# When the next head's adding transfers start, and when the output projections' rows are loaded and split

## The chip, the cores and the metric

The kernel runs on one core of a Trainium2 chip. The metric is the device time of one execution in microseconds (us). Five engines work side by side, each on its own list of instructions, in order: TensorE (PE: matrix products; PEld is its loading of weights), VectorE (DVE), ScalarE (ACT), GpSimd (POOL) and SyncE (SP), which here only issues transfers. GpSimd and ScalarE issue transfers too. The order of each list is made when the kernel is built; when the instructions run is settled by semaphores.

## What is computed

Two decoder layers on 512 tokens of width 2048, in float32. The first layer is differential attention with 8 heads, the second a gated RWKV-7. Both end in an output projection that is added to the input:

```python
def diff_attention_mixer(h, cos, sin, w_in, q_gain, k_gain, ..., w_out, lambda_init):
    proj = h @ w_in                       # 512 x 2048 by 2048 x 8192
    q, k, v, gate = jnp.split(proj, 4, axis=-1)
    ...
    q = apply_rope(rms_norm(q, q_gain), cos, sin)
    k = apply_rope(rms_norm(k, k_gain), cos, sin)
    ...
    o = causal_diff_attention(q, k, v, lam)
    o = rms_norm(o, subln_w) * (1.0 - lambda_init)
    o = o.reshape(B, T, DA_WIDTH).astype(h.dtype) * jax.nn.silu(gate)
    return o @ w_out
...
def rwkv7_mixer(...):
    p = h @ w_in
    ...
    y = wkv7_scan(rh, heads(decay), kh, vh, -kk, kk * ah)
    ...
    y = y.reshape(B, T, RW_WIDTH).astype(h.dtype) * jax.nn.silu(g)
    return y @ w_out, v_first
...
for i in range(DEPTH):                    # DEPTH = 2
    hn = rms_norm(x, norm_w[i])
    x = x + (diff_attention_mixer(...) if i % 2 == 0 else rwkv7_mixer(...)[0])
```

## The kernel before

**Splits.** Every product is made of three matmuls on halves: a value is rounded to a high half by a cast on ScalarE, and VectorE subtracts it from the value to give the low half. For weights, `split_w` does this (lines 109 and 110) or, in the first layer's heads, `Seven.split` (lines 600 and 601: `wh`, `wl`). Rows of the left side are split by `split_row` (lines 474 and 475: `hH`, `hL`). Weights are loaded as raw tiles (`wraw`, three buffers, 512 KB for two blocks of 128 rows) by SyncE; four buffers each hold high and low halves.

**A head of the first layer.** `Seven.head` makes the projection of one head (heads 1 to 7; head 0 goes another way) with products on sums of weight blocks in place of some plain products. A weight sum is made by transfers: SyncE loads one block into a tile, then GpSimd issues a transfer that adds another block to it in memory (`fetch` with `add=True`, line 571; plain loads are line 573). Six pairs of blocks of such sums live in the tile `T`; they carry the next head's first product. `prime(h + 1)` loads `T` by SyncE in three groups (512 KB each), `prime(h + 1, True)` adds to it by GpSimd, three transfers again.

The end of a head runs as follows, in the program's order. The S1 product: three groups, each a raw tile loaded by SyncE and added to by GpSimd. Then the combining step of line 640 (`take`, on VectorE, at a higher priority than the splits). Then the first group of the S4 product, with its own raw tile (the "first S4 load"). Then, for heads 1 to 6, `prime(h + 1, True)`, the three adding transfers for the next head, inside `tc.issue_after(g.m.ins)`, where `g.m` is the last matmul. Then the plain products on blocks 12 and 13, and 14 and 15, each pair from one raw tile. Then the other two groups of S4.

`tc.issue_after(ins)` puts the instructions that it encloses behind `ins` in the list of the engine of `ins`: only those that are on that engine. `high_priority` moves instructions ahead in the order that the builder chooses.

While a head's products run, the attention of the head before is interleaved by a `Chain`: after so many matmuls (`delay`, then the step's own gap) it issues its next step. In the attention, scores go to `sc`, line 415 makes the weights `p` on VectorE, line 421 turns them on TensorE, line 445 turns the result `yt`.

**The output projections.** `unit_tok` multiplies 16 rows of the attention's result (16 blocks of 128 by 512 tokens) with `w_out`, in 8 weight groups of two blocks, 24 matmuls a group, and calls `more(n, m)` three times in each group, with growing `n`. The rows lie in device memory (`yd`, `yd2`). Before, `split_rows` loads and splits 14 rows ahead of the projection: it issues a load and a split for each row in one go. In the first layer, rows 0 to 3 and 8 to 11 go through parts of `Tt` (the place of `T`), the others through four `t1` tiles, and splits from row 8 on stand behind the last gate's instructions. The last head's attention runs meanwhile (`Chain` with delay 4, gap 21; seven steps); it gives rows 14 and 15. In the second layer the rows go through eight tiles of one buffer each, and the last pair's recurrence runs meanwhile.

The rest of both projections uses sums again (`sum_forms`, `seven`) and isn't touched.

Of the kernel before, what the change touches and what calls it, by code (L numbers as in the profile page):

```python
# [13 lines left out]
F32 = mybir.dt.float32  # L14
# [9 lines left out]
P = 128  # L24
D = 2048
T = 512
KT = D // P
NT = T // P
NH = 8
# [51 lines left out]
class Halves:  # L81


    def __init__(self, parts, n):
        self.parts, self.n = parts, n
# [5 lines left out]
@urgent  # L91
def split_w(g, block, kg, cols, k0, raw=None):


    nc = g.nc
    held = raw is not None and block is not None
    if raw is None:
        raw = g.wraw.tile([P, kg, cols], F32, name="wraw", tag="wraw")
        load_w(g, raw, block, k0, slice(0, kg))
    n = kg // 2  # L100
    his, los = [], []
    for k in range(0, kg, n):
        hi = g.wh.tile([P, n, cols], F32R, name="wh", tag="wh")
        lo = g.wl.tile([P, n, cols], F32R, name="wl", tag="wl")
        with ExitStack() as after:
            if held and k0 + k < 4:
                for ins in g.made[k0 + k - 1] if k0 + k else [g.made_prm]:
                    after.enter_context(g.tc.issue_after(ins))
            nc.scalar.copy(hi[:], raw[:, k : k + n])  # L109
            nc.vector.tensor_sub(lo[:], raw[:, k : k + n], hi[:].bitcast(F32))  # L110
        his.append(hi)
        los.append(lo)
    return Halves(his, n), Halves(los, n)
# [356 lines left out]
def split_row(g, yr):  # L470
    nc = g.nc
    hh = g.hp.tile([P, T], F32R, name="hH", tag="hH")
    hl = g.hp.tile([P, T], F32R, name="hL", tag="hL")
    nc.scalar.copy(hh[:], yr)
    g.rowsplit = nc.vector.tensor_sub(hl[:], yr, hh[:].bitcast(F32)).ins
    return hh, hl


def split_rows(g, src, tags, bufs, n=KT, late=KT, behind=(), first=()):

    out = []
    for k in range(n):
        i = k % (2 * len(first)) if first else k
        yr = first[i] if i < len(first) else g.work.tile([P, T], F32, name="yr", tag=tags[k % len(tags)], bufs=bufs)[:]
        g.nc.sync.dma_start(out=yr, in_=src[k * P : (k + 1) * P, :])
        with ExitStack() as after:
            for ins in behind if k >= late else ():
                after.enter_context(g.tc.issue_after(ins))
            out.append(split_row(g, yr))
    return out  # L490


class Tokens:
# [24 lines left out]
class Seven:  # L518
# [3 lines left out]
    def __init__(self, g, aps):  # L522
        self.g, self.made = g, 0
        self.win = aps["da_w_in"]
        tags = [t for t in LOW for _ in range(LOW[t])]
        self.S = {n: [g.low.tile([P, 2, 2, 256], F32R, name=n, tag=t, bufs=LOW[t]) for t in tags[3 * i : 3 * i + 3]]
                  for i, n in enumerate(("S1", "S2", "S4"))}
        self.T = g.work.tile([P, KP, 512], F32, name="T", tag="T", bufs=1)
# [50 lines left out]
    def raw(self, n, k0, half, h, also=None):  # L579

        with self.ahead:
            raw = self.g.wraw.tile([P, n, 512], F32, name="wraw", tag="wraw")[:]
            self.fetch(raw, k0, half, h)
            if also:
                self.fetch(raw, *also, h, add=True)
        return raw
# [6 lines left out]
    def split(self, raw):  # L593

        g, out = self.g, []
        with self.ahead:
            for k in range(raw.shape[1]):
                hi = g.wh.tile([P, 512], F32R, name="wh", tag="wh")
                lo = g.wl.tile([P, 512], F32R, name="wl", tag="wl")
                g.nc.scalar.copy(hi[:], raw[:, k])  # L600
                g.nc.vector.tensor_sub(lo[:], raw[:, k], hi[:].bitcast(F32))  # L601
                out.append((hi, lo))
        return out
# [38 lines left out]
    def head(self, h):  # L642

        g, A, B, U, W, T = self.g, self.A, self.B, self.U, self.W, self.T
        top, low = (lambda k: self.rows(k, 0)), (lambda k: self.rows(KP + k, 0))
        tile_of = lambda k, n: T[:, k : k + n]
        more = lambda k0, half: lambda k, n: self.add(k, n, k0, half, h)
        q = QK(g)
        self.product(B, lambda k: self.rows(k, 1), h, tile_of, True, then=more(0, 0))
        self.product(A, top, h, lambda k, n: self.raw(n, k, 0, h), True)  # L650
        self.copy(W, B)
        self.product(B, low, h, lambda k, n: self.raw(n, KP + k, 0, h), True, end=False)
        self.copy(q.t1s[:2], A)
        self.product(A, lambda k: self.form("S2", k), h, tile_of, False, then=more(KP, 0), end=False)
        self.copy(U, A)
        self.plain(0, h, ((0, B, False, True), (1, A, False, False)))
        self.take(q.t1s[:2], q.t1s[:2], B)
        self.product(A, lambda k: self.rows(KP + k, 1), h, tile_of, False)
        if h + 1 < NH:
            self.prime(h + 1)  # L660
        for t in range(2):
            rope(g, q, t)
        self.take(q.t1s[2:], A, W)
        self.product(B, lambda k: self.form("S1", k), h, lambda k, n: self.raw(n, k, 0, h, (k, 1)), True)
        for t in range(2, NT):
            rope(g, q, t)
        norm_qk(g, q)
        qkT = head_qkT(g)
        Chain(g, keys(g, q, qkT, 10), 52)
        last = lambda k, n: self.raw(n, KP + k, 1, h)  # L670
        s4 = lambda k: self.form("S4", k)
        self.take(U, B, U, ALU.subtract)
        self.product(A, s4, h, last, True, GROUPS[:1])
        if h + 1 < NH:
            with g.tc.issue_after(g.m.ins):
                self.prime(h + 1, True)
        self.plain(1, h, ((0, A, False, False), (1, B, True, True)))
        self.take(W, U, W, ALU.subtract)
        self.product(A, s4, h, last, False, GROUPS[1:])
        vg = VG(g)  # L680
        for c in list(g.chains):
            c.finish(g)
        self.take(W, W, B)
        self.take(U, U, A)
        with g.tc.high_priority(offset=AHEAD if h == NH - 1 else 0):
            for t, x in ((2, W[0]), (3, W[1]), (0, U[0]), (1, U[1])):
                vg.convert(g, t, x)
        return qkT + (q.sq, vg)
# [151 lines left out]
def layer0(g, aps):  # L840
# [3 lines left out]
    with ExitStack() as cx:  # L844
# [22 lines left out]
        with tc.high_priority(offset=AHEAD):  # L867
            xs += [xp.tile([P, NT, 512], F32, name=f"x{cb}") for cb in range(4)]
            g.first += [(g.wraw.tile([P, 2, 512], F32, name="wraw", tag="wraw"), i == 0) for i in range(3)]
            at = lambda k, n: (xs[k // 4], slice(k * P, (k + n) * P), slice(k % 4 * P, (k % 4 + n) * P))  # L870
            load_x(*at(0, 1))
            warmed = warm_up(5)
            g.prm_a = load_rows(g, [(0, 32, aps["norm_w"].rearrange("l (k p) -> (l k) p", p=P))], 32, nc.scalar)
            first = load_first(0, slice(0, 1), nc.scalar)
            on = g.const.tile([P, 1], F32, name="on")
            nc.vector.memset(on[:], 0.0)
            with tc.issue_after(first):
                nc.scalar.copy(on[:], on[:])
            load_x(*at(1, 1))
            load_first(0, slice(1, 2))  # L880
            load_x(*at(2, 1))
            load_first(2, slice(0, 2))
            load_x(*at(3, 1))
            load_x(*at(4, 2))
            load_first(4, slice(0, 2))
            for k in range(6, KT, 2):
                load_x(*at(k, 2))
# [39 lines left out]
    with ExitStack() as cx:  # L927
# [16 lines left out]
            Chain(g, attention(g, h - 1, *before, 37), 28 if h > 1 else 1)  # L944
            before = u.head(h)
        Tt = g.work.tile([P, KP, 512], F32, name="Tt", tag="T", bufs=1)
        rows = split_rows(g, g.yd, ("t1",), 4, KT - 2, 8, g.gated, [Tt[:, k] for k in range(4)])
        ch = Chain(g, attention(g, NH - 1, *before, 21, rows, Tt[:, 4:6]), 4)

        def all_rows(n, _):  # L950
            if n >= KT - 1:
                ch.finish(g)

# [694 lines left out]
def layer1(g, aps):  # L1648
    nc, tc = g.nc, g.tc
    with ExitStack() as cx:  # L1650
# [74 lines left out]
                gated(g, j - 1, pairs[j - 1], gts[0], True)  # L1725

        gts.append(gate(g, j, proj(3, j, behind=[(24, last_but_one)]), "E"))
        rows = split_rows(g, g.yd2, ("r", "k", "th0", "th1", "l", "f", "xH", "xL"), 1, j - 1)

        def all_rows(n, _):  # L1730
            if n >= 4 and len(rows) == KT - 2:
                rows.append(split_row(g, gts[0][:]))
            if n >= KT and len(rows) < KT:
                p.chain.finish(g)
                finish_y(g, j, p)
                gated(g, j, p, gts[1], True)
                rows.append(split_row(g, gts[1][:]))
# [110 lines left out]
```

## Time and profile before

| | us |
|---|---|
| three runs, median | 2096.42 |
| lowest, highest | 2092.53, 2097.5 |
| profiled execution, its own time | 2097.94 |
| its span in the profile | 2096.2 |
| TensorE busy | 2071.3 |
| VectorE busy | 1663.4 |
| ScalarE busy | 1250.0 |
| GpSimd busy | 401.8 |

The profile is of one execution, and its span is counted from its first to its last instruction. In a row of a group or a timeline stand start and duration in us, the engine, the line of the kernel, the operation and, as out<-in, the tiles that it writes and reads; in brackets the idle time of the engine before it and what ended that. In a list of waits stand the total, the number and the longest. "SPq" and the like mean the queue of an engine that issues transfers. The granted TensorE clock was 0.998 of full speed. Heads 1 to 7 take the stretch from about 97 to 750 us, the first layer's output projection begins at 750, the second layer's ends the span.

### The profile page before, as it was taken

The numbers are of one execution on the slowest core, as the hardware profiler recorded it, in microseconds if no ns is written. First come the engines' busy times: TensorE is split into PE (matmuls) and PEld (weight loads), VectorE is DVE, ScalarE is ACT, GpSimd is POOL, SyncE is SP. The second block draws the span as 40 slices with busy tenths as digits, with TensorE's granted clock in tenths as the row PEclk, the third lists the DMA queues.
The fourth block names the chain that finished last, engine by engine and source line by source line (L and its number), as shares of the span: only waits on it lengthen the run. The fifth ranks groups of instructions, "written<-read, shape, count | busy, mean of one in ns | idle before, by whom it ended". The sixth has DMA issues, their size and how long they took to land.

```text
span 2096.2 us, 35298 instructions
## 1 busy us (share of the span) xinstructions
PE 2071.3 (99%) x12008; PEld 1708.4 (81%) x12008; DVE 1663.4 (79%) x4353; ACT 1250.0 (60%) x3005; POOL 401.8 (19%) x698
## 2 busy tenths in 40 slices
PE   9999999999999999999999999999999999999999
PEld 8888878888887878888778888888888888877887
DVE  5978777787877886576888888888888888887645
ACT  5766665666666664446666666666666666655333
POOL 0110101101010000101233332233333322343001
PEclk9999999999999999999999999999999999999999
DMA  6577868677776766652212222222222222245565
GB/s 200 147 181 178 188 177 196 165 188 179 184 189 181 176 228 198 167 117 93 83 55 79 79 81 71 87 79 79 79 79 79 78 77 75 85 129 173 194 162 119
DMA packets 101781, 280.71 MB, mean 134 GB/s; under 512 B 12544, under 2 KB 29072, under 8 KB 101600
## 3 DMA queue, kind: packets, MB, share of 16 engines
q1 hardware_dynamic: 68064, 198.90, 29.3%
q0 software_dynamic: 19104, 63.55, 16.5%
q10 hardware_dynamic: 14432, 16.01, 2.2%
q8 instruction: 94, 1.54, 0.3%
q14 instruction: 87, 0.71, 0.1%
HBM read 262.42 MB, written 15.99 MB: 133 GB/s over the span
## 4 chain that ended last, share of the span: by engine, by line
PE 86%; DVE 7%; ACT 2%; DMA 2%; issue 1%; POOL 0%; ACTq 0%; DVEq 0%; POOLq 0%
PE pp L118 65%; PE pt L118 6%; DMA wraw<-in_da_w_in_dram 2%; PE gp L1340 1%; PE sc L118 1%; PE sm L1559 1%; PE sm L1581 1%; PE lora L118 1%; DVE wl L601 1%; PE sm L1572 1%; PE o L118 1%; PE z L118 1%; DVE wl L110 1%; PE Y L1605 1%; PE pt L359 1%
## 5 line engine op out<-in xcount | busy, mean ns | idle before, releaser
L118 PE MATMUL pp<-hH,wh 128*128 128x512 f32 x1024 | 416.7, 407 | 0.0
L118 PE MATMUL pp<-hL,wh 128*128 128x512 f32 x1024 | 412.3, 403 | 0.0
L118 PE MATMUL pp<-hH,wl 128*128 128x512 f32 x1024 | 411.8, 402 | 0.0
L109 ACT CAST wh<-wraw 128x512 fp32r<-128x512 f32 (+1 forms) x412 | 253.9, 617 | 198.4 <-PE pp L118 100.0
L118 PE MATMUL pp<-wl,hH 128*128 128x512 f32 x932 | 365.9, 393 | 4.2 <-DVE wl L601 4.2
L118 PE MATMUL pp<-wh,hH 128*128 128x512 f32 x932 | 366.7, 394 | 0.5 <-ACT wh L600 0.5
L110 DVE TENSOR_TENSOR wl<-wraw,wh 128x512 fp32r<-128x512 f32 (+1 forms) x412 | 286.0, 695 | 101.4 <-ACT wh L109 97.1
L118 PE MATMUL pp<-wh,hL 128*128 128x512 f32 x932 | 365.6, 392 | 0.0
L118 PEld LDWEIGHTS pp<-hH,wh 128*128 128x128 f32 x1024 | 192.8, 188 | 37.8 <-issue 2.3
L118 PEld LDWEIGHTS pp<-hH,wl 128*128 128x128 f32 x1024 | 193.1, 189 | 32.9
L118 PEld LDWEIGHTS pp<-hL,wh 128*128 128x128 f32 x1024 | 193.2, 189 | 31.3
L118 PEld LDWEIGHTS pp<-wl,hH 128*128 128x128 f32 x932 | 175.2, 188 | 42.4 <-DVE wl L601 7.6
L118 PEld LDWEIGHTS pp<-wh,hH 128*128 128x128 f32 x932 | 175.1, 188 | 36.8 <-ACT wh L600 1.9
L118 PEld LDWEIGHTS pp<-wh,hL 128*128 128x128 f32 x932 | 175.1, 188 | 35.7
L600 ACT CAST wh<-wraw 128x512 fp32r<-128x512 f32 x224 | 138.4, 620 | 105.5 <-PE pp L118 69.0
L601 DVE TENSOR_TENSOR wl<-wraw,wh 128x512 fp32r<-128x512 f32 x224 | 151.5, 687 | 51.9 <-ACT wh L600 51.3
L1567 POOL COPY SA<-VS 64x64 f32<-64x64 f32 x224 | 75.7, 338 | 520.9 <-DVE VS L1585 464.5
L118 PE MATMUL pp<-wh,S 128*128 128x512 f32 x504 | 162.7, 394 | 0.0
L571 POOL DMA_DIRECT2D T<-in_da_w_in_dram x63 | 53.8, 869 | 493.2 <-DVE wl L601 400.8
L1433 DVE SCALAR_TENSOR_TENSOR tmpl<-LT,n,Tm 128x60 f32<-128x60 f32 (+24 forms) x496 | 135.5, 273 | 13.3
L1436 DVE TENSOR_TENSOR Tm<-Tm,tmpl 128x60 f32<-128x60 f32 (+24 forms) x496 | 105.7, 213 | 13.6
L600 ACT CAST wh<-T 128x512 fp32r<-128x512 f32 x126 | 77.8, 618 | 54.0 <-PE pp L118 53.8
(372 smaller groups left out, 3971.0 us busy)
## 6 DMA issues: line engine op xcount, KB each, us to landing
wraw<-in_rw_w_in_dram SPq DMA_DIRECT2D x128, 512.0 KB, 3.7
wraw<-in_da_w_in_dram SPq DMA_DIRECT2D x127, 512.0 KB, 4.3
T<-in_da_w_in_dram POOLq DMA_DIRECT2D x63, 512.0 KB, 6.6
wraw<-in_da_w_out_dram SPq DMA_DIRECT2D x26, 512.0 KB, 4.4
wraw<-in_rw_w_out_dram SPq DMA_DIRECT2D x26, 512.0 KB, 4.0
T<-in_da_w_in_dram SPq DMA_DIRECT2D x21, 512.0 KB, 6.4
wraw<-in_da_w_in_dram POOLq DMA_DIRECT2D x21, 512.0 KB, 7.4
yr<-yd SPq DMA_DIRECT2D x20, 256.0 KB, 3.3
```

The source lines that it names most:

```text
L109: nc.scalar.copy(hi[:], raw[:, k : k + n])
L110: nc.vector.tensor_sub(lo[:], raw[:, k : k + n], hi[:].bitcast(F32))
L118: m = nc.tensor.matmul(out, a, b, start=s, stop=e, skip_group_check=skip)
L359: nc.tensor.transpose(pt[:, c * P : (c + 1) * P], t1s[t][:, c * P : (c + 1) * P], g.ident[:])
L571: self.g.nc.gpsimd.dma_start(out=raw, in_=src, accum_op=ALU.add)
L600: g.nc.scalar.copy(hi[:], raw[:, k])
L601: g.nc.vector.tensor_sub(lo[:], raw[:, k], hi[:].bitcast(F32))
L1340: m = nc.tensor.matmul(gp[h][:, i * P : (i + 1) * P], BK[r_, c0 + i, :, :], p.AR[r_, c0 + i, :, :], start=True, stop=True)
L1433: st = nc.vector.scalar_tensor_tensor(tt, LT[:, i : i + 1, i + 1 :].to_broadcast([P, s, n]), n2[:, i : i + 1], Tm[:, 0:s, i : i + 1].to_br ...
L1436: nc.vector.tensor_add(Tm[:, 0:s, i + 1 :], Tm[:, 0:s, i + 1 :], tt)
L1559: nc.tensor.matmul(sm[:, 0:P], both(p.G[:, c, 0]), both(VS[:, c]), start=True, stop=True)
L1567: nc.gpsimd.tensor_copy(p.SA[r_, c - 1, :], VS[r_, c, h, :])
```

## The change

First, in the heads: the program remembers the last raw tile that was fetched (`self.fetched`; where it is used, the first S4 load). Ahead of the next head's three adding transfers, GpSimd copies one column of that tile into a small tile (`mark`, 128 by 1, which nothing else needs by then), and the transfers are put behind this copy, on the same engine, in place of behind a matmul. So the copy waits until the tile has landed, and the transfers wait for the copy.

Second, in both output projections: `split_rows` gives way to a class `Feed`. It loads six rows and splits four at the start; at each call of `more(n, m)` it splits on to row n + 1 and loads on to row n + 7, and VectorE's part of these splits is put behind the last weight split (`g.split`). With n = 2, 3, 4 in the first group and 4, 5, 6 in the second, the rest of the 14 rows is split from the first to the fifth weight group. The first layer's condition on the last gate is gone. The last attention's delay is 12 instead of 4 and its gap 22 instead of 21.

```diff
-            nc.vector.tensor_sub(lo[:], raw[:, k : k + n], hi[:].bitcast(F32))
+            g.split = nc.vector.tensor_sub(lo[:], raw[:, k : k + n], hi[:].bitcast(F32)).ins
...
-def split_rows(g, src, tags, bufs, n=KT, late=KT, behind=(), first=()):
-
-    out = []
-    for k in range(n):
-        i = k % (2 * len(first)) if first else k
-        yr = first[i] if i < len(first) else g.work.tile([P, T], F32, name="yr", tag=tags[k % len(tags)], bufs=bufs)[:]
-        g.nc.sync.dma_start(out=yr, in_=src[k * P : (k + 1) * P, :])
-        with ExitStack() as after:
-            for ins in behind if k >= late else ():
-                after.enter_context(g.tc.issue_after(ins))
-            out.append(split_row(g, yr))
-    return out
+class Feed:
+    def __init__(self, g, src, n, home):
+        self.g, self.src, self.n, self.home, self.raw, self.rows = g, src, n, home, [], []
+        self.load(6)
+        self.split(4)
+
+    def load(self, upto):
+        for k in range(len(self.raw), min(upto, self.n)):
+            self.raw.append(self.home(k))
+            self.g.nc.sync.dma_start(out=self.raw[k], in_=self.src[k * P : (k + 1) * P, :])
+
+    def split(self, upto, after=None):
+        for k in range(len(self.rows), min(upto, self.n)):
+            with self.g.tc.issue_after(after) if after else ExitStack():
+                self.rows.append(split_row(self.g, self.raw[k]))
+
+    def __call__(self, n):
+        self.split(n + 2, self.g.split)
+        self.load(n + 8)
...
             self.fetch(raw, k0, half, h)
+            self.fetched = raw
...
         if h + 1 < NH:
-            with g.tc.issue_after(g.m.ins):
+            landed = g.nc.gpsimd.tensor_copy(self.mark[:], self.fetched[:, 0, 0:1])
+            with g.tc.issue_after(landed.ins):
                 self.prime(h + 1, True)
...
-        rows = split_rows(g, g.yd, ("t1",), 4, KT - 2, 8, g.gated, [Tt[:, k] for k in range(4)])
-        ch = Chain(g, attention(g, NH - 1, *before, 21, rows, Tt[:, 4:6]), 4)
+        feed = Feed(g, g.yd, KT - 2, lambda k: g.work.tile([P, T], F32, name="yr", tag="t1", bufs=4)[:] if k & 4 else
+                    Tt[:, k % 4])
+        rows = feed.rows
+        ch = Chain(g, attention(g, NH - 1, *before, 22, rows, Tt[:, 4:6]), 12)
 
         def all_rows(n, _):
+            feed(n)
             if n >= KT - 1:
                 ch.finish(g)
...
-        rows = split_rows(g, g.yd2, ("r", "k", "th0", "th1", "l", "f", "xH", "xL"), 1, j - 1)
+        feed = Feed(g, g.yd2, KT - 2, lambda k: w.tile([P, T], F32, name="yr", bufs=1, tag=(
+            "r", "k", "th0", "th1", "l", "f", "xH", "xL")[k % 8])[:])
+        rows = feed.rows
 
         def all_rows(n, _):
+            feed(n)
             if n >= 4 and len(rows) == KT - 2:
                 rows.append(split_row(g, gts[0][:]))
```

More of the change, by code (lines that the diff above doesn't have):

```diff
@@ L524, in __init__ @@
         self.win = aps["da_w_in"]
+        self.mark = g.on
         tags = [t for t in LOW for _ in range(LOW[t])]
@@ L876, in layer0 @@
             nc.vector.memset(on[:], 0.0)
+            g.on = on
             with tc.issue_after(first):
```

## The prediction

> **What bounds the kernel now.** I read the page first, for which engine sets the end, then what TensorE waits for, then the chain of waits head by head.
>
> ```profile
> span 2096.2 us, 35298 instructions
> ...
> PE 2071.3 (99%) x12008; PEld 1708.4 (81%) x12008; DVE 1663.4 (79%) x4353; ACT 1250.0 (60%) x3005; POOL 401.8 (19%) x698
> ...
> PE 86%; DVE 7%; ACT 2%; DMA 2%; issue 1%; POOL 0%; ACTq 0%; DVEq 0%; POOLq 0%
> ...
> wraw<-in_da_w_in_dram SPq DMA_DIRECT2D x127, 512.0 KB, 4.3
> ```
>
> The kernel is bound by TensorE: 99% busy, 86% of the chain. The edit takes no matmul away, so all it can change is the moments in which TensorE waits. The 2% of DMA in the chain says that some of these are loads. The last row is the time from issue to landing that half of the weight loads stay under, 4.3 us. TensorE's own waits, over the whole span:
>
> ```profile
> PE pp L118 <- DVE wl L601: 4.6, 10, 0.8
> ...
> PE pp L118 <- ACT wh L600: 0.5, 2, 0.4
> ```
>
> Line 601 makes the low half of a weight block in the first layer's heads. Ten waits, 4.6 us: the profile counts only what lies beyond the modelled end of the matmul before, so the delay is larger. To see it whole I use the chain, where one long piece returns once a head (heads 2 to 7), with the longest loads between:
>
> ```profile
> 156.24 8.44 PE pp L118 x37
> ...
> 206.29 6.66 PE pp L118 x29
> ...
> 261.03 8.29 DMA wraw<-in_da_w_in_dram
> ...
> 298.87 6.66 PE pp L118 x29
> ...
> 391.62 6.66 PE pp L118 x29
> ...
> 483.79 6.66 PE pp L118 x29
> ...
> 535.07 7.19 DMA wraw<-in_da_w_in_dram
> ...
> 575.00 6.66 PE pp L118 x29
> ...
> 667.35 6.66 PE pp L118 x29
> ```
>
> The first row gives the pace: 8.44/37 = 0.228 us a matmul. The others give five heads (2 to 6): 92.58, 92.75, 92.17, 91.21, 92.35 us. Same work, yet head 5 is shorter by 1.37, 1.54, 0.96 and 1.14 than the rest: 5.0 us together. Each head's chain runs through one load far over 4.3 us. What TensorE did there, in head 2 and in head 5:
>
> ```profile
> 270.06 0.49 PE L118 MATMUL pp<-wh,hH 128*128 128x512 f32 x1 [0.16 <-ACT wh L600]
> ...
> 273.19 0.50 PE L118 MATMUL pp<-wl,hH 128*128 128x512 f32 x1 [0.75 <-DVE wl L601]
> ...
> 548.57 0.39 PE L118 MATMUL pp<-wh,hH 128*128 128x512 f32 x1
> 549.28 0.50 PE L118 MATMUL pp<-wl,hH 128*128 128x512 f32 x1 [0.32 <-DVE wl L601]
> ```
>
> Head 5 is not clean either: its matmul starts 0.71 after the one before, 0.48 over the pace, and runs 0.50 instead of 0.39; 0.6 us lost. So a head without the waits is 90.6 us, and five heads lose 5.0 + 5 x 0.6 = 8.0 us. Who was late in head 2, on ScalarE and VectorE:
>
> ```profile
> 269.39 0.62 ACT L600 CAST wh<-wraw 128x512 fp32r<-128x512 f32 x1 [1.03 <-DMA wraw<-in_da_w_in_dram]
> ...
> 270.04 0.69 DVE L601 TENSOR_TENSOR wl<-wraw,wh 128x512 fp32r<-128x512 f32 x1 [1.01 <-ACT wh L600]
> 270.65 0.68 DVE L640 TENSOR_TENSOR u<-pp,u 128x512 f32<-128x512 f32 x1
> 271.25 1.28 DVE L640 TENSOR_TENSOR u<-u 128x512 f32<-128x512 f32 x2
> 272.45 1.89 DVE L601 TENSOR_TENSOR wl<-wraw,wh 128x512 fp32r<-128x512 f32 x3
> ```
>
> The load of blocks 12 and 13 (issued 261.03) lands at 269.3. The cast of block 12 waits for it; the three combining steps of line 640 stand on VectorE between the splits of blocks 12 and 13, so the second split slips too. What shares the engines with that load:
>
> ```profile
> q0 software_dynamic: 450, 1.61, 43.7%
> q1 hardware_dynamic: 821, 3.01, 42.5%
> ...
> wraw<-in_da_w_in_dram SPq DMA_DIRECT2D x4, 512.0 KB, 7.3
> T<-in_da_w_in_dram POOLq DMA_DIRECT2D x3, 512.0 KB, 8.9
> ...
> 251.78 0.85 POOL L571 DMA_DIRECT2D T<-in_da_w_in_dram  x1 [8.20 <-DVE rs_t L68]
> 254.77 0.85 POOL L571 DMA_DIRECT2D T<-in_da_w_in_dram  x1 [2.14 <-DVE wl L601]
> 260.59 0.85 POOL L571 DMA_DIRECT2D T<-in_da_w_in_dram  x1 [4.97 <-DVE rs_t L67]
> 288.19 0.85 POOL L571 DMA_DIRECT2D T<-in_da_w_in_dram  x1 [26.75 <-DVE wl L601]
> ...
> 257.57 17.13 SPq L573 DMA_DIRECT2D wraw<-in_da_w_in_dram  x6
> ```
>
> These are DMA queues and issues between 250 and 271 us, then GpSimd's and SyncE's timelines. The queues are full (43.7 + 42.5%, ACT's and others beside). The three adding transfers for head 3 take 43.7% x 21 / 3 = 3.1 us of all engines each; a plain load 42.5% x 21 / 6 = 1.5. They go out at 251.78, 254.77 and 260.59, around the first S4 load (257.57) and the load of blocks 12 and 13. Nobody reads their result before the next head: the split of its first group ends just before 288.19.
>
> **The change, part by part.** *The wait.* The old order behind a matmul doesn't hold GpSimd's transfers: that matmul is the last of the first S4 group, just before 270.06, and in the rows above they leave at 251.78 to 260.59. The new copy reads the raw tile of the first S4 load, so the three adding transfers follow its landing. Without them this load takes some 4.3 us: 257.57 + 4.3 = 261.9 (in head 5 this load is the 7.19 us row). Behind the copy on GpSimd stand only the three transfers, then those of 288.19. The nearest row to the copy's cost is GpSimd's copy in the second layer:
>
> ```profile
> L1567 POOL COPY SA<-VS x224: 227/233/1159, 1039.6 to 1934.2; 64x64 f32<-64x64 f32 x112
> ```
>
> 0.23 us at the median, 1.16 at most, for 64 columns where the new one has one; I take 0.23. It lies on GpSimd, which is idle there, so its cost is nothing while VectorE isn't touched. The adds then leave from 262.1 to 263.8 and, at 8.9 us, land by about 274 of the 288 when they are needed: 14 us of cover. The raw buffer is held until the copy has read it, which is before the cast does.
>
> The load of blocks 12 and 13, issued at 261.03 as before, takes 4.3 alone and up to another 1.5 if it shares half the engines: 265.3 to 266.8. When must it land? Undisturbed, block 13's low half is needed at 269.74 + 7 x 0.228 = 271.3 (269.74: the matmul before 270.06 at the pace). Ahead of it on VectorE come split, three steps and split, 4 x 0.6 + 0.69 = 3.1, and the cast, 0.6: landing by 267.6. So both waits go. Bounds: 8.0 saved; at the other end the waits only move. I take 8.0.
>
> The Trainium skill, in "DMA: Bandwidth & Descriptors", section "Queues, rings and completion order", says that each DMA engine takes turns between queues, packet by packet. By that rule a load can't be put behind whole adding transfers, and the sum stays at 8.0; the two nearly equal shares above agree with it, though they don't prove it. A rule speaks against the change: the Trainium skill, "SBUF — State Buffer", section "Who interferes with whom", says that a VectorE instruction with two SBUF inputs and a GpSimd instruction that reads SBUF can't run together. By it, each of six copies could hold up a weight split by its own 0.23, 1.4 us in all, and the sum of this part would be 6.6; no run here shows it, since GpSimd does no arithmetic in these heads.
>
> *Output projection, first layer.* Same fourteen rows, same splits, same loads; moved are rows 6 to 13 on SyncE and rows 4 to 13 on VectorE, behind the weight splits. What TensorE waits for between 700 and 800 us that this touches, then one row each of ScalarE's, VectorE's and TensorE's timelines:
>
> ```profile
> PE pt L421 <- DVE p L415: 1.5, 1, 1.5
> PE yt L445 <- DVE rho L413: 0.5, 1, 0.5
> ...
> 751.48 0.62 ACT L474 CAST hH<-yr 128x512 fp32r<-128x512 f32 x1 [1.95 <-DMA yr<-yd]
> ...
> 793.38 1.29 DVE L475 TENSOR_TENSOR hL<-Tt,hH 128x512 fp32r<-128x512 f32 x2 [1.87 <-ACT hH L474]
> ...
> 800.68 0.39 PE L118 MATMUL pp<-wh,hH 128*128 128x512 f32 x1
> ```
>
> ScalarE stands 1.95 us before a row's cast, with the last head's work queued behind it, and ten row splits crowd VectorE just when the attention's first block needs it: 2.0 us on TensorE. With two rows per weight group that crowd goes. The attention starts 8 matmuls later and each of six rounds is one longer: 14 x 0.228 = 3.2 us later at its end. Its last two rows are split by 794.7 and first used at 800.68, so 2.8 us of cover stay. Bounds: 2.0 saved, to 2.0 lost if a paced split now holds up a block instead. I take 1.5 saved, since the cause named in the row is moved away.
>
> *Second layer.* The same move; between 1900 and 1960 us TensorE's waits are one:
>
> ```profile
> PE sm L1559 <- DVE VS L1585: 0.2, 1, 0.2
> ```
>
> I take 0, bounds 0.2 saved to 2.0 lost (as above).
>
> **Sum.** 8.0 + 1.5 = 9.5. The profiled run took 2097.94 us, 1.5 over the median of the three, so 2088.4 for it and 2086.9 for the median: I say 2087.0.
>
> **The rivals.**
>
> *Half of it.* The loads come early but VectorE's order still puts three steps before block 13's split, as in head 5, which waits for that split alone (549.28). Saved 5.0, and 1.0 in the projection: 2090.4. For it: head 5. Against it: head 5's VectorE was late from the start, its chain going through the first S4 load (535.07, 7.19 us), which the change relieves. 0.18.
>
> *The waits only move.* The adds weren't what was slow, or the S4 load lands so early that they leave as before. Saved 0 to 2: about 2095. Against it: the 43.7% of the engines' time that they take. 0.08.
>
> *Slower: three adds at once in front of the loads TensorE needs next.* They used to be 9 us apart and now leave within 1.7 us of each other, just behind the load of blocks 12 and 13. If that load has to wait for whole adds, it lands at 265.3 + 3.1 for each: with one, 268.4, still before 269.3; from two on later than now, 271.5, and with three 274.6, by 2.2 and 5.3 us a head, 11 to 26 over five heads, less 1.5: 2106 to 2121; I say 2108. It decides from the point where the load waits for more than 1.3 adds. For it: loads of 7.3 us in the median above. Against it: the load is issued about 1 us ahead of the first add. 0.12.
>
> **How the numbers follow.** The forecast has 0.62. A measurement can tell 0.3% from no change, 6.3 us: 2090.1. The forecast counts as faster; of the half case, at 2090.4, 0.08 as faster and 0.10 as same; the moved waits as same; the last as slower. Faster 0.70, same 0.18, slower 0.12. Range: down to 8.0 + 2.0 + 0.2 and the 2.5 us half width of the runs before, 2083.5; up to 2096.5, which takes in the half case and the moved waits and leaves out the slower one.
>
> **What would show it.** Right: heads 2 to 6 all near 90.6 us; GpSimd's copy at the landing of the first S4 load and three adding transfers right behind; loads of blocks 12 and 13 landing within 6 us; the waits on line 601 nearly gone; no 1.5 us wait on line 415. Wrong: heads of 91 to 92 with waits on line 601 behind line 640 (half of it), or loads of 8 us and more behind the adds (slower), or a new wait for rows or for the attention between 750 and 806 us.

## The result: slower by 0.3%, and the profile after

| | before | after |
|---|---|---|
| median us (11 runs each, on one chip) | 2096.11 | 2100.86 |
| lowest, highest | 2091.62, 2098.62 | 2096.65, 2105.11 |
| span of the profiled execution | 2096.2 | 2098.1 |

The ratio is 1.0029, 95% interval 1.0019 to 1.0039 (an estimate over all runs; the two medians alone give 1.0023). So the kernel is slower by 4 to 8 us, where I had forecast 9.4 faster: 2087.0, and 2096.5 at most. In the code of after, lines 600 and 601 have become 612 and 613, 640 has become 652, 571 and 573 have become 582 and 584; the new copy is line 687.

The page of after, against the rows shown of before:

```profile
span 2098.1 us, 35310 instructions
...
PE 2071.4 (99%) x12008; PEld 1706.5 (81%) x12008; DVE 1664.4 (79%) x4353; ACT 1248.9 (60%) x3005; POOL 402.7 (19%) x704
...
PE 83%; DVE 9%; ACT 3%; DMA 3%; issue 2%; SPq 0%; ACTq 0%; DVEq 0%
```

TensorE is as busy as before, but its share of the chain fell from 86% to 83%, and VectorE, ScalarE and DMA each have more of it. TensorE's own waits between 90 and 700 us, where the heads lie (in total, times, longest):

```profile
PE pt L359 <- ACT t L326: 5.9, 6, 1.5
PE pt L359 <- DVE qkL L363: 1.9, 6, 0.3
PE pp L118 <- DVE wl L613: 0.2, 1, 0.2
```

The waits on the splits, 4.6 us before over the whole span, are down to 0.2, as forecast. In their place TensorE stands at line 359, which transposes the normalised queries and keys: once in each of heads 2 to 6 for line 326 on ScalarE (it scales the keys by their norm), and once in each of heads 1 to 6 for line 363. The sixth wait on line 326, of 0.7 us, lies ahead of head 1 and is there before the change too. The chain of waits, with the long piece that returns once a head (heads 1 to 7) and the longest load of heads 1 and 2:

```profile
116.91 6.66 PE pp L118 x29
...
172.63 8.71 DMA wraw<-in_da_w_in_dram
...
207.84 6.66 PE pp L118 x29
...
265.04 9.18 DMA wraw<-in_da_w_in_dram
...
300.42 6.66 PE pp L118 x29
...
392.87 6.66 PE pp L118 x29
...
485.88 6.66 PE pp L118 x29
...
578.70 6.66 PE pp L118 x29
...
671.96 6.66 PE pp L118 x29
```

Heads 2 to 6 take 92.58, 92.45, 93.01, 92.82 and 93.26 us; 90.6 was forecast, and before had 91.21 to 92.75. Head 1 took 89.21 before; its long piece in before's chain stands at

```profile
117.08 6.66 PE pp L118 x29
```

and the next at 206.29. It now takes 90.93. Heads 1 to 6 together are 4.8 us longer, as much as the medians differ (4.75). The two spans differ by 1.9 only: the first output projection gives back 0.7, and before's profile has a loss of 1.25 at the passage between the layers that only e1's and e2's show too.

The load on the chain is now that of blocks 14 and 15. From it, the chain of head 2 runs like this:

```profile
265.04 9.18 DMA wraw<-in_da_w_in_dram
...
274.30 0.63 ACT wh L612
274.93 0.02 issue
274.95 1.29 DVE wl L613 x2
276.25 0.34 DVE t L310
...
277.73 0.64 DVE t L313
...
279.64 0.68 DVE wl L613
...
280.86 0.18 DVE rr L321
281.04 0.02 issue
281.07 0.41 ACT t L326
281.48 0.04 issue
281.52 0.62 PE pt L359 x2
```

VectorE's list holds both splits of that load, then the last ropes (lines 310 to 313, the rotation of queries and keys by their position) and the key normalisation (to line 321); ScalarE's line 326 waits for these. All of it is late because the load is. GpSimd's timeline and the DMA issues from 263 to 265.2 us (number, KB, median us to landing) show what the load met:

```profile
262.78 0.62 POOL L687 COPY on<-wraw 128x1 f32<-128x1 f32 x1 [17.08 <-DMA wraw<-in_da_w_in_dram]
263.34 2.61 POOL L582 DMA_DIRECT2D T<-in_da_w_in_dram  x3
```

```profile
T<-in_da_w_in_dram POOLq DMA_DIRECT2D x3, 512.0 KB, 10.8
wraw<-in_da_w_in_dram SPq DMA_DIRECT2D x1, 512.0 KB, 9.2
```

The copy runs when the first S4 load has landed, and all three adding transfers leave from 263.34 on, ahead of the load at 265.04. The load of blocks 12 and 13, issued 0.8 us ahead of them, took 3.5 us.

### The profile page after: what moved, and what is told of

It reads as the page before. It is cut to its first block, busy times and chain, and to the rows that moved or that the text cites. A ratio compares the mean times of both kernels' runs of the same rounds, so it can differ in the third digit from the quotient of the medians.

```text
span 2098.1 us, 35310 instructions
## 1 busy us (share of the span) xinstructions
PE 2071.4 (99%) x12008; PEld 1706.5 (81%) x12008; DVE 1664.4 (79%) x4353; ACT 1248.9 (60%) x3005; POOL 402.7 (19%) x704
## 4 chain that ended last, share of the span: by engine, by line
PE 83%; DVE 9%; ACT 3%; DMA 3%; issue 2%; SPq 0%; ACTq 0%; DVEq 0%
PE pp L118 62%; PE pt L118 6%; DMA wraw<-in_da_w_in_dram 3%; DVE wl L613 2%; PE gp L1357 1%; PE sc L118 1%; PE sm L1576 1%; PE sm L1598 1%; PE lora L118 1%; PE sm L1589 1%; PE o L118 1%; PE z L118 1%; PE Y L1622 1%; DVE wl L110 1%; PE pt L359 1%
```

## The experiments

**What is asked.** Theory A: three adds released together keep the DMA engines busy for some 15 us (in head 2 the first is issued at 263.34 and the third lands at 278.79), the load of blocks 14 and 15 comes late, and the ropes and the key normalisation stand behind its splits. Rivals: the copy itself costs something, the rows of the output projection cost something, or an added wait is bad wherever it stands. e1, e6 and e8 are edits of the kernel before, the others of the kernel after. In this table the heads are read as above, from the piece of 29 matmuls: "head 1" from its first to its second return, and the mean of heads 2 to 6 from the second to the seventh.

| kernel | median us | ratio to before, 95% | head 1 | mean of heads 2 to 6 |
|---|---|---|---|---|
| before | 2096.11, 2094.17, 2094.27, 2095.13 in four sets of runs | | 89.21 | 92.21 |
| after | 2100.86 | 1.0029 (1.0019 to 1.0039) | 90.93 | 92.82 |
| e1, wait alone | 2098.69 | 1.0024 (1.0015 to 1.0033) | 90.48 | 92.88 |
| e2, rows alone | 2093.74 | 0.9995 (0.9986 to 1.0004) | 89.40 | 91.80 |
| e3, wait behind 14 and 15 | 2086.90 | 0.9966 (0.9953 to 0.9978) | 89.21 | 90.55 |
| e4, a wait for each add | 2087.83 | 0.9971 (0.9960 to 0.9983) | 89.24 | 90.81 |
| e5, ropes and norm ahead | 2097.07 | 1.0009 (1.0001 to 1.0017) | 90.47 | 92.33 |
| e6, copies alone | 2093.43 | 0.9994 (0.9986 to 1.0002) | 90.24 | 92.27 |
| e7, no such adds | 2086.30 | 0.9957 (0.9944 to 0.9970) | 89.22 | 90.55 |
| e8, as e3, rows as before | 2086.11 | 0.9955 (0.9943 to 0.9967) | 89.21 | 90.55 |
| e9, e3 with e5's order | 2095.82 | 1.0005 (0.9996 to 1.0015) | 90.45 | 91.93 |
| e10, two adds early | 2097.89 | 1.0013 (1.0003 to 1.0024) | 89.79 | 92.39 |
| e11, one add early | 2086.73 | 0.9962 (0.9947 to 0.9976) | 89.43 | 90.60 |

**e1: the copy and its wait alone**, on the kernel before.

```diff
             self.fetch(raw, k0, half, h)
+            self.fetched = raw
...
         if h + 1 < NH:
-            with g.tc.issue_after(g.m.ins):
+            landed = g.nc.gpsimd.tensor_copy(self.mark[:], self.fetched[:, 0, 0:1])
+            with g.tc.issue_after(landed.ins):
                 self.prime(h + 1, True)
```

> The copy and the wait alone; the rows as in the kernel before. Theory A (the three adding transfers, let go together, take the DMA engines from the load of blocks 14 and 15, and the key normalisation stands behind that load's cast and split on ScalarE and VectorE): 3 to 6 us slower than before, heads of 92.4 to 93.3 us, waits on line 326. Theory B (the rows' part is what costs): 6 to 9 us faster than before.

Slower by 0.15 to 0.33%, with the same waits of TensorE in the heads as after:

```profile
PE pt L359 <- ACT t L326: 6.3, 6, 1.6
PE pt L359 <- DVE qkL L363: 1.9, 6, 0.3
```

Within the intervals, the whole loss lies in this part of the change.

**e2: the output projections' part alone** (the changed kernel with the old wait).

```diff
-            landed = g.nc.gpsimd.tensor_copy(self.mark[:], self.fetched[:, 0, 0:1])
-            with g.tc.issue_after(landed.ins):
+            with g.tc.issue_after(g.m.ins):
```

> The rows loaded and split a few at a time alone; the adding transfers as in the kernel before. Theory A: 1 to 3 us faster than before (the two traces differ by 0.75, 1.25 and 0.45 us in the stretches that hold rows), heads as before. Theory B: 3 to 6 us slower than before.

No difference that can be told: the interval runs from 2.9 us faster to 0.8 slower. That rules out theory B, but not theory A's 1 to 3 us. TensorE's waits between 700 and 800 us:

```profile
PE pt L421 <- DVE p L415: 1.7, 1, 1.7
PE yt L445 <- DVE y L440: 0.5, 1, 0.5
```

The 1.5 us wait on line 415 that I had put down to crowded row splits is still there with the rows spread out.

**e3: the copy reads the tile of blocks 14 and 15 instead**, so that the adds follow that load.

```diff
         self.product(A, s4, h, last, True, GROUPS[:1])
+        self.plain(1, h, ((0, A, False, False), (1, B, True, True)))
         if h + 1 < NH:
             landed = g.nc.gpsimd.tensor_copy(self.mark[:], self.fetched[:, 0, 0:1])
             with g.tc.issue_after(landed.ins):
                 self.prime(h + 1, True)
-        self.plain(1, h, ((0, A, False, False), (1, B, True, True)))
```

> As the changed kernel, but the copy reads the raw tile of blocks 14 and 15 in place of the first S4 load's, so the adding transfers leave behind both loads. Theory A: heads of 90.4 to 91 us with neither the waits on line 601's splits nor those on line 326, 8 to 11 us faster than before. Theory C (the copy itself costs, by the port it shares with VectorE or by holding the raw tile): heads as in the changed kernel, 3 to 6 us slower than before.

Faster than before by 7.3 us at the median, a little under the 8 to 11 expected. The chain through head 2, where after had the load and its splits, is TensorE's alone:

```profile
263.43 0.22 PE yt L445 x2
263.65 15.02 PE pp L118 x66
278.67 0.44 PE pt L359 x4
```

The load of blocks 14 and 15 took 3.6 us here, and VectorE's timeline has the last ropes from 271.05 on:

```profile
271.05 0.42 DVE L310 TENSOR_TENSOR t<-t,ropeS 128x256 f32<-128x256 f32 x1
```

The adds now meet the two loads behind it, and slow these as much (issues from 269.5 to 271.5 us):

```profile
wraw<-in_da_w_in_dram SPq DMA_DIRECT2D x2, 512.0 KB, 10.4
```

But those loads have more time, and TensorE doesn't wait for them. What matters is which load meets the adds. That an added wait is bad wherever it stands has fallen.

**e4: a copy and a wait for each add**, behind the first S4 load, the load of blocks 12 and 13, and that of 14 and 15.

```diff
-            self.fetched = raw
+            self.fetched.append(raw)
...
+        self.plain(1, h, ((0, A, False, False), (1, B, True, True)))
         if h + 1 < NH:
-            landed = g.nc.gpsimd.tensor_copy(self.mark[:], self.fetched[:, 0, 0:1])
-            with g.tc.issue_after(landed.ins):
-                self.prime(h + 1, True)
-        self.plain(1, h, ((0, A, False, False), (1, B, True, True)))
+            for (k, n), raw in zip(GROUPS, self.fetched[-3:]):
+                landed = g.nc.gpsimd.tensor_copy(self.mark[:], raw[:, 0, 0:1])
+                with self.ahead, g.tc.issue_after(landed.ins):
+                    self.fetch(self.T[:, k : k + n], k, 1, h + 1, True)
```

> As the changed kernel, but each of the three adding transfers has a copy of its own: the first reads the first S4 load's tile, the second that of blocks 12 and 13, the third that of blocks 14 and 15. Theory A: the transfers no longer leave together, the load of blocks 14 and 15 meets at most one or two of them: 5 to 10 us faster than before, heads of 90.4 to 91.5. Theory C: three times as many copies, 5 us slower than before or more.

Nearly as good as e3, with heads of 90.55 to 91.31 us. In head 2 the load of blocks 14 and 15 takes 7.3 us, and next to nothing of that reaches TensorE (90.69 us).

**e5: the last two ropes and the key normalisation ahead of the splits**, the early wait kept.

```diff
-        for t in range(2, NT):
-            rope(g, q, t)
-        norm_qk(g, q)
+        with g.tc.high_priority(offset=SCAN):
+            for t in range(2, NT):
+                rope(g, q, t)
+            norm_qk(g, q)
```

> As the changed kernel, but the turning of the last two token blocks and the key normalisation have the priority of the combining steps, so that on VectorE the last turning stands ahead of the splits of blocks 14 and 15. The loads land as late as in the changed kernel. Theory A1 (the late load costs because the key normalisation stands in VectorE's list behind that load's splits): the waits on line 326 shrink to less than half, heads of 90.5 to 91.5 us, 3 to 8 us faster than the changed kernel. Theory A2 (the late load would hold up the matmuls themselves): waits on line 613 or on casts take their place, within 2 us of the changed kernel.

The waits on line 326 are gone from the heads, and as many on the splits stand there:

```profile
PE pp L118 <- DVE wl L613: 6.3, 6, 1.1
```

By itself this reads as a late load that costs much the same whoever stands behind it, though by the ratios e5 is some 0.2% faster than after. e9 puts that right.

**e6: the copies alone**, behind the adds, holding nothing.

```diff
             self.fetch(raw, k0, half, h)
+            self.fetched = raw
...
             with g.tc.issue_after(g.m.ins):
                 self.prime(h + 1, True)
+            g.nc.gpsimd.tensor_copy(self.mark[:], self.fetched[:, 0, 0:1])
```

> The kernel before with the six copies, which stand behind the adding transfers and hold up nothing. Theory A: the copies cost nothing, within 2 us of before. Theory C (the shared port, or the raw tile held longer): slower than before by 3 us or more.

No slower than before: six copies cost at most 0.4 us (0.02%), so the copy is not the cause.

**e7: the prime's adding transfers left out.**

```diff
-        if h + 1 < NH:
-            landed = g.nc.gpsimd.tensor_copy(self.mark[:], self.fetched[:, 0, 0:1])
-            with g.tc.issue_after(landed.ins):
-                self.prime(h + 1, True)
```

> The changed kernel without the three adding transfers for the next head (18 in all; that part of the weight sums is left out). Theory A: this is the floor of the heads, 90.5 us each, and the kernel with the later wait has reached it: 2086 to 2088 us, within 1.5 us of that one. If the adds still cost something where the wait is later, this one is faster than it by 2 us or more.

This is the floor: 90.55 us for each of heads 2 to 6, and no wait of TensorE in them. The medians of e3 and e8 lie within 0.6 us of it while these two do all the work.

**e8: the later wait of e3 with the rows as before.**

```diff
             self.fetch(raw, k0, half, h)
+            self.fetched = raw
...
+        self.plain(1, h, ((0, A, False, False), (1, B, True, True)))
         if h + 1 < NH:
-            with g.tc.issue_after(g.m.ins):
+            landed = g.nc.gpsimd.tensor_copy(self.mark[:], self.fetched[:, 0, 0:1])
+            with g.tc.issue_after(landed.ins):
                 self.prime(h + 1, True)
-        self.plain(1, h, ((0, A, False, False), (1, B, True, True)))
```

> The later wait alone, rows as in the kernel before. Theory A: 6 to 8 us faster than before, within 1.5 us of the kernel that has both, as the rows' part is worth 0.4 us. If the rows' part is worth more beside undisturbed heads, this one is slower than the one with both by 2 us or more.

The lowest median of the kernels that compute everything, 8.2 us under the runs of before beside it and, by the two ratios (0.9955 and 1.0029), 0.7% under after; it is level with e3: here too no gain of the rows' part can be told.

**e9: e3 with e5's order**, the control that e5 lacked: the edit of e5 on the kernel e3.

> The wait behind blocks 14 and 15 (no late load in front of the key normalisation), with the last two ropes and the key normalisation moved ahead of the weight splits as in the run before that did so. Theory L (the waits on the splits in that run came from the late load): heads 2 to 6 at 90.55 us, no waits on line 613, 2086 to 2087 us. Theory R (the new order makes them itself, since the ropes now stand in front of the splits): heads of 91 to 92 us, waits on line 613 of 3 to 6 us in the heads, 2089 to 2095 us.

Theory R holds, with a median and waits just above its ranges. With no late load, each of heads 2 to 6 takes 91.9 us, and the waits are those of e5:

```profile
PE pp L118 <- DVE wl L613: 6.3, 6, 1.1
```

The chain of its head 2 has no load in it:

```profile
269.30 0.59 DVE u L652
269.89 0.60 DVE t L312
...
271.09 0.68 DVE t L313
271.78 0.15 DVE rs_i L64
271.93 0.54 DVE wl L613
272.47 0.04 issue
272.51 8.46 PE pp L118 x36
```

The ropes now hold up a split: e5's waits are the price of its order, not of the load. Against its own control e5 loses 2.0 us over heads 2 to 6 (0.4 a head), where after loses 11.4 against e3 (2.3 a head). The late load costs mostly through the ropes and the key normalisation behind it. As e9's heads are 1.4 us longer, they also give the load that much more time; a loss that reached TensorE by another way would then still be 0.9 a head.

**e10 and e11: two adds early, and one**, the rest behind the load of blocks 14 and 15. Here e10:

```diff
             with g.tc.issue_after(landed.ins):
-                self.prime(h + 1, True)
+                for k, n in GROUPS[:2]:
+                    self.add(k, n, 0, 1, h + 1)
         self.plain(1, h, ((0, A, False, False), (1, B, True, True)))
+        if h + 1 < NH:
+            landed = g.nc.gpsimd.tensor_copy(self.mark[:], self.fetched[:, 0, 0:1])
+            with g.tc.issue_after(landed.ins):
+                for k, n in GROUPS[2:]:
+                    self.add(k, n, 0, 1, h + 1)
```

> Dose: two of the three adding transfers follow the first S4 load as in the changed kernel, the third follows the load of blocks 14 and 15. Measured so far for the load of blocks 14 and 15: 3.6 us with no add ahead of it, 9.2 with three. Theory Q (the load is slowed by the adds' work that is queued ahead of it, so by their number): 7 to 8 us, heads of 90.8 to 91.6, 2088 to 2093 us. Theory S (the load shares with the adding queue turn by turn, so that one add that is under way is as bad as three, as long as it lasts past the load): 8.5 to 9.5 us, heads of 92 to 93, 2096 to 2101 us.

> Dose: one of the three adding transfers follows the first S4 load, the other two follow the load of blocks 14 and 15. Theory Q: the load of blocks 14 and 15 takes 5 to 6.5 us, less than its slack of some 3.5 us over 3.6; heads at 90.55 to 90.7, 2086 to 2088 us. Theory S: 7 to 9 us, heads of 91 us and more, 2089 to 2098 us.

The load of blocks 14 and 15 in head 2, first in e11, then in e10 (DMA issues around it):

```profile
wraw<-in_da_w_in_dram SPq DMA_DIRECT2D x1, 512.0 KB, 6.0
```

```profile
wraw<-in_da_w_in_dram SPq DMA_DIRECT2D x1, 512.0 KB, 8.8
```

With no add ahead of it the load takes 3.6 us, then 6.0 with one, 8.8 with two, 9.2 with three. One add is nearly free: heads 2 to 6 stay at 90.55, but for one of 90.78, and head 1 is 0.2 longer than in e3. Two cost most of what three do (1.8 us a head over the floor in heads 2 to 6, against 2.3), and TensorE's waits are back:

```profile
PE pt L359 <- ACT t L326: 3.1, 5, 1.5
PE pt L359 <- DVE qkL L363: 1.6, 5, 0.3
```

Neither theory held throughout: from none to two the number counts, as Q says; from two to three hardly, as S says. The load lands 0.5 us after the first add in e11, 0.2 before the second in e10, and 0.5 before the second of three in after.

The traces hold a closer check. Take heads 2 to 6 of after, e1, e3, e4, e7, e8, e10 and e11, 40 heads in all, and set each head's time beside its own load of blocks 14 and 15. Where the load takes up to 6.8 us, the head takes 90.55 or 90.56. Beyond 7.1 us the head is longer by what the load takes over 7.1, to within 0.12 us: a load of 7.90 goes with a head of 91.31 (e4), 8.80 with 92.22 (e10), 9.83 with 93.26 (after). So the load has some 3.5 us to spare, and what exceeds that reaches TensorE one for one.

## Why the prediction was wrong

**Right: where before lost its time.** The floor was put at 90.6 us a head and the loss of heads 2 to 6 at 8.0 us; e7 and e8 give 90.55, and e8 gains 8.2 us at the median. The adds around the first S4 load and the loads behind it were the cause.

**Right: the first steps.** The copy ran at the landing of the first S4 load, three adds right behind it; that load and the next landed 3.6 and 3.5 us after their issue (4.3, and up to 5.8 for the second, were allowed), and the waits on the splits went.

**The step that failed: "14 us of cover".** I followed the adds to the one load issued just ahead of them, and then to their reader in the next head. Between the two stand other loads; that of blocks 14 and 15, issued at 265.04, 1.7 us behind the first add, was never followed, nor what VectorE holds behind its splits. So the sum has no term for a load that is issued while the adds run. That load took 5.6 us longer than in e3 (9.2 for 3.6), of which some 3.5 were to spare, and it cost 2.0 us in head 2. The adds were also put too short: the third was to land by about 274 and landed at 278.79, 14.4 us after its issue, where 8.9 was the median of adds that left one by one. Their reader in the next head did have cover, as forecast (289.93).

**The slower rival had the mechanism, on the wrong load, and its price too high.** It named three adds in front of loads that TensorE needs next, but was priced on blocks 12 and 13, and I set it low since that load leaves 1 us ahead of the adds. That order excused one load; the next one paid. In head 1 even the order was not so: there the load of blocks 12 and 13 left 0.7 us behind the first add and took 6.9. In head 2, of 5.6 us some 3.3 are left where the ropes begin on VectorE (276.17 against 271.05 in e3, less the 1.8 by which head 2 begins later, 207.84 against 206.01), and 2.0 at the head's end. As the kernel before already lost 1.7 a head, the net is small: 4.8 us over six heads, not 11 to 26.

**"The waits only move" came true in a way it didn't say:** the waits did move, from the splits to line 359, but because the early adds meet the next load, not because they weren't what was slow.

**Head 1 was left out.** It had nothing to gain in before's profile and lost 1.7 us, over a third of the whole loss. That its 89.21 was clean is partly that one profile's luck: in e6, with the adds where they were, it took 90.24.

**The rows: 1.5 saved was taken, 0.4 measured, not distinguishable from nothing** (e2; e8 against e3). The cause "named in the row" wasn't: line 421 still waits with the rows paced, 1.7 us in e2 and 1.3 in after.

**The copy.** Taken at 0.23 us, it took 0.62 in head 2 and 0.19 to 0.72 over the six heads, on an engine that had the time. In heads 2 to 6 it ends 0.04 or 0.05 us behind a split of line 613 on VectorE: in head 2 the split runs from 262.67 to 263.36 and the copy to 263.40. With nothing on VectorE beside it, it takes 0.19 (e4, at 270.36). The rule quoted from the Trainium skill, "SBUF — State Buffer", section "Who interferes with whom", that two such instructions can't run together, agrees with this. But here it is the copy that waits, not the split: the 1.4 us that the prediction worked out for VectorE didn't show, as e6's interval ends at 0.4 us.

**The turns.** I held the load of blocks 12 and 13 to 1.5 us more at worst, for engines shared by halves. On the load of blocks 14 and 15 the extra was 2.4 us with one add and 5.6 with three. With three, it landed ahead of the second and the third, so it didn't stand behind whole adds. The rule of the Trainium skill, "DMA: Bandwidth & Descriptors", section "Queues, rings and completion order", that an engine takes turns between queues packet by packet, agrees with that. But it gave me no bound on the time: a load that alone took 3.6 us took 9.2. Whether the turns are unequal in time, or what else makes the load land with the second add, no run here tells.

**A slip in the range.** Its lower end adds up to 2083.7, not 2083.5; nothing rests on it.

## What to carry to other kernels

When background transfers are moved, list every load issued until they have all landed, and for each what is queued behind its consumer; here the load issued just ahead of the adds was spared, and the next one paid. Compare what a load takes with what it may take (here 7.1 us) before moving anything in front of it. Put the transfers behind the last load whose list is tight (here that of blocks 14 and 15: a ratio of 0.9955, against 1.0024 behind the first S4 load), or release only as many as that load can bear (here one of three). And an experiment that moves work ahead of other work needs its own control: without e9, e5 would have been read the wrong way.

## What the runs showed of the hardware

In head 2 the load of 512 KB took 3.6 us on its own, 6.0 behind one adding transfer of the same size, 8.8 behind two and 9.2 behind three. Over heads 2 to 6 it took 3.4 to 3.6 (e3), 5.8 to 7.2 (e11), 8.5 to 9.9 (e10) and 9.0 to 9.8 (after): the third is nearly free to the load, the first two are not.

A copy of one column on GpSimd took 0.19 us alone and up to 0.74 (e6) where it met a split on VectorE, and then ended just behind that.

Where adds meet loads as in the kernel before, one profile's heads differ more: in e2 heads 2 to 6 run from 90.57 to 92.88 us, in e3, e7 and e8 all are 90.55 or 90.56. Whether the spread between whole runs is smaller there too isn't shown: 0.7, 2.8 and 3.9 us over 5, 6 and 5 runs of e8, e7 and e3 stand against 10.2 over 23 runs of before, but a range grows with the number of runs.
